# A hybrid block (window attention, RWKV-7, retention, FFN): norm factors moved to the keys, rotation in one product, in-context rate kept as its tanh, key scale on ScalarE

## Chip, cores and metric

One core of one Trainium2 chip. The metric is device time in microseconds (us) of one execution, the median of the runs shown. TensorE (PE) multiplies matrices, VectorE (DVE) and ScalarE (ACT) work elementwise, GpSimd (POOL) does a few small powers, SyncE (SP) issues the loads. A core has an on-chip memory of 128 partitions; TensorE writes its sums to PSUM.

## The reference

Two layers over 256 tokens of width 1024, float32. In each layer one projection feeds three branches, whose outputs are gated, mixed, projected and added to the input; a gated FFN follows. Cut to what the change touches:

```python
def hybrid_layer(x, ...):
    h = _rms(x) * norm1_g
    aq, ak, av, rw, rq, rk, rv, rg, gates = _split(h @ w_in, IN_SIZES)
    aq = _rms(aq.reshape(B, T, 8, 64)) * attn_q_norm_g      # 8 query heads
    ak = _rms(ak.reshape(B, T, 2, 64)) * attn_k_norm_g      # 2 key heads
    o_a = sliding_window_attention(aq, ak, av, attn_sinks) @ w_attn_o
    o_b = rwkv7_time_mix(rw, ...) @ w_rwkv_o
    o_c = retention(rq, rk, rv, rg) @ w_ret_o
    ...
def rwkv7_time_mix(h, ...):
    ...
    a = jax.nn.sigmoid(a0 + ad @ a2)                        # in-context rate
    kk = (k * k_k); kk = kk / max(norm_per_head(kk), 1e-12)
    k = k * (1.0 + (a - 1.0) * k_a)                         # key scale
    # per step: S = S*w + (S @ -kk) * (kk*a) + v*k ; y = S @ r
    ...
def _rotary(x, pos):                                        # on rq and rk
    x1, x2 = x[..., :32], x[..., 32:]
    return concat([x1 * cos - x2 * sin, x2 * cos + x1 * sin])
```

The attention's scores are products of a query and a key, so a factor per element of the head can stand on either of them. The sigmoid is written as 0.5 + 0.5 tanh of half its argument.

## The kernel before

**Tiling.** Tokens come in two halves of 128 (`t`). Every weight is brought in as a unit of 128 x 1024 numbers (`raw`, 512 KB), split by ScalarE into a rounded part `wh` and by VectorE into the rest `wl`, and multiplied in three products (high by high, high by low, low by high), which keeps float32 accuracy. Three buffers each hold `raw`, `wh` and `wl`.

**Streams.** The big products form one chain in program order (called bulk): attention's queries `aq` and keys and values `akv`, the rwkv columns `pf`, retention's `rq`, `rv`, `rg`, `rk`, the gates `gt`, the branches' output products `po` (attention, then retention, then rwkv), `px`, and the FFN's `pfg`, `pfu`, `pd`. Beside it run the attention (stream 3), the rest of rwkv (stream 1), the retention (stream 2) and the mixing (stream 4).

**Order.** Nothing is issued in program order. `Program` records every operation; `schedule` and `forward` simulate the five queues from a table of costs (`cost`) and latencies, and pick on each engine the ready operation with the highest key; `emit` then writes that order out, so all instructions carry line 432 in the profile and are told apart by their tiles. The key puts due weights first, then the longest remaining path (with the costs of stream 1 counted 2.5 times), and lets bulk products fill the rest. An engine works through its own queue strictly in order. The costs that meet the change:

```python
if eng == "DVE":
    ...
    if method in ("tensor_copy", "tensor_scalar", "memset") and not src:
        return 150 + n / 1.92
    return (210 if method == "scalar_tensor_tensor" else 150) + n / 0.96
if eng == "ACT":
    c = (155 if src else 200) + n / 1.2
    if _is_ap(kw.get("scale", 1.0)) or _is_ap(kw.get("bias", 0.0)):
        c += 95
```

**Buffers.** Tiles of a pool are handed out in program order: `s` (4 buffers of work space: `q_sb`, `asq`, `ask`, `qn`, `t1`, `t2` and others), `m` (5 buffers: the attention's `aqs`, `sc`, `pT`, then the retention's `rqT`, `rkT`, `sT`), `r` (14, mostly rwkv), `k` (5), and 4 PSUM buffers each for bulk and for the rest.

**Attention, for each t.** `q_sb` is the query, evicted from PSUM with the row's scale; ScalarE squares it, VectorE sums the squares per head, GpSimd raises them to -1/2 (`arq`). Two VectorE products write `qn`, the query times its norm's factor with the heads regrouped (pairs of a head of each key group side by side); TensorE transposes `qn` (`pta`). The keys get their row's factor and their norm's factor in `kv`. `qng` holds both norm factors of both layers, spread over the partitions by four loads. Scores `sc`, their maximum `amx`, the exponentials with their sums, the reciprocal `adn` of the denominator, the transposes `ptp` into `pT` and the product `poa` follow.

**Rotation.** `rope` evicts to `q_sb`, multiplies by cosines into `t1` (one product of 512) and by signed sines into `t2` (two products of 256, each reading the other half of every head); the sum is transposed into `rqT` or `rkT`. Then come `pst`, `sT`, `po`, the square `rsq`, its sums `rvr`, the power on GpSimd and its scale (`rrr`), two products `o`, and the transposes `ptc` into `och` and `ocl`, which the bulk product with `w_ret_o` reads.

**Rwkv.** `na` is the tanh of the in-context rate from ScalarE, turned by one VectorE operation of 1024 numbers a partition into minus the rate (-0.5 tanh - 0.5). After the key's norm (`kq`, `pss`, `ssm`, `rin`, `kkn`), four VectorE operations write `k2` = `na` * `nka` + `oka` (shown in the profile as `k`), then come `k2` * `zk`, `na` * `kkn`, the decays `EN`, the operands `X`, and a triangular inverse of 31 steps on VectorE (`prod`, `Tt`).

Of the kernel before, what the change touches and what calls it, by code (L numbers as in the profile page):

```python
# [439 lines left out]
def hybrid_kernel(ctx: ExitStack, tc: tile.TileContext, A: dict, cst_d: bass.AP, out: bass.AP, layers=L):  # L440
# [64 lines left out]
    def bcast_rows(src, n, o):  # L505
        return bass.AP(tensor=src.tensor, offset=src.offset + o, ap=[[0, 128], [1, n]])
# [142 lines left out]
    hw = TL(cp, [128, 16], F32, name="hw")  # L649
    ts(hw, vec[:, 28:44], 0.5, None, MUL)  # L650
    nka = TL(cp, [128, 8], F32, name="nka")
    ts(nka, vec[:, vo["ka"]:vo["ka"] + 8], -1.0, None, MUL)
    oka = TL(cp, [128, 8], F32, name="oka")
    ts(oka, vec[:, vo["ka"]:vo["ka"] + 8], -1.0, 1.0, MUL, ADD)
    qng = TL(cp, [128, 2, 2, 64], F32, name="qng")
    snk = TL(cp, [128, 16], F32, name="snk")
    for l in range(L):
        dma(out=qng[:, l, 0, :], in_=bcast_rows(A["attn_q_norm_g"], 64, l * 64))
        dma(out=qng[:, l, 1, :], in_=bcast_rows(A["attn_k_norm_g"], 64, l * 64))
    dma(out=snk, in_=bcast_rows(A["attn_sinks"], 16, 0))  # L660


# [7 lines left out]
    for l in range(layers):  # L670
# [23 lines left out]
        def rope(ps, t):  # L694
            q = ST([128, 512], "q_sb")
            act(q, ps[t], AF.Copy, scale=rs[:, t:t + 1])
            t1 = ST([128, 512], "t1")
            cosb = bc(C("cos")[:, t * 32:(t + 1) * 32].unsqueeze(1), [128, 16, 32])
            tt(t1.rearrange("p (a b) -> p a b", b=32), q.rearrange("p (a b) -> p a b", b=32), cosb, MUL)
            t2 = ST([128, 512], "t2")  # L700
            q4 = q.rearrange("p (h s b) -> p h s b", s=2, b=32)
            t24 = t2.rearrange("p (h s b) -> p h s b", s=2, b=32)
            for s in range(2):
                sinb = bc(C("sin")[:, t * 64 + s * 32:t * 64 + (s + 1) * 32].unsqueeze(1), [128, 8, 32])
                tt(t24[:, :, s, :], q4[:, :, 1 - s, :], sinb, MUL)
            return t1, t2

        def rope_T(ps, dstT, keep=None):
# [16 lines left out]
        for t in range(2):  # L725
            q = ST([128, 512], "q_sb")
            kv = TL(z_p, [128, 256], F32, tag="kv", name="kv")
            act(q, psq[t], AF.Copy, scale=rs[:, t:t + 1])
            act(kv, psk[t], AF.Copy, scale=rs[:, t:t + 1])
            av.append(kv)  # L730
            sq = ST([128, 512], "asq")
            ss = TL(sm_p, [128, 10], F32, tag="ass", name="ass")
            act(sq, q, AF.Square)
            V.tensor_reduce(out=ss[:, 0:8], in_=sq.rearrange("p (h v) -> p h v", h=8), axis=AX.X, op=ADD)
            sk = ST([128, 128], "ask")
            act(sk, kv[:, 0:128], AF.Square)
            V.tensor_reduce(out=ss[:, 8:10], in_=sk.rearrange("p (h v) -> p h v", h=2), axis=AX.X, op=ADD)

            ts(ss[:, 0:8], ss[:, 0:8], 64e-6, None, ADD)
            ts(ss[:, 8:10], ss[:, 8:10], 1.0 / 64, 1e-6, MUL, ADD)  # L740
            rq_ = TL(sm_p, [128, 10], F32, tag="arq", name="arq")
            G.tensor_tensor(out=rq_, in0=ss, in1=C("mh")[:, :10], op=ALU.pow)
            q3 = q.rearrange("p (h v) -> p h v", h=8)
            rqs.append(rq_)
            qn = ST([128, 512], "qn")
            qn4 = qn.rearrange("p (g k v) -> p k g v", g=4, k=2)
            for kvh in range(2):
                tt(qn4[:, kvh], q3[:, kvh * 4:kvh * 4 + 4, :], bc(qng[:, l, 0:1, :], [128, 4, 64]), MUL)
            k3 = kv[:, 0:128].rearrange("p (h v) -> p h v", h=2)
            tt(k3, k3, bc(rq_[:, 8:10].unsqueeze(2), [128, 2, 64]), MUL)  # L750
            tt(k3, k3, bc(qng[:, l, 1:2, :], [128, 2, 64]), MUL)
            pt = PS([128, 512], "pta")
            transposes(pt, qn)
            p4 = pt.rearrange("p (k t) -> p k t", k=4)
            for kvh in range(2):
                r_, q_ = HR[kvh], HR[1 - kvh]
                S.copy(qs[t][r_, kvh], p4[r_])
                tt(qs[t][q_, kvh], p4[r_], qs[t][r_, kvh].bitcast(F32), SUB)
            pt = PS([128, 128], "ptk")
            P.transpose(pt, kv[:, 0:128], ident)  # L760
            tk = slice(t * 128, (t + 1) * 128)
            for kvh in range(2):
                r_, q_ = HR[kvh], HR[1 - kvh]
                S.copy(ks[r_, kvh, tk], pt[r_])
                S.copy(ks[q_, kvh, tk], pt[r_])
                tt(klz[r_, kvh, tk], pt[r_], ks[r_, kvh, tk].bitcast(F32), SUB)
# [73 lines left out]
        for u in (6, 2, 3, 0, 1, 4, 5):  # L840
            pf = [PG([128, T], "pf") for _ in range(2)]
            for kg in range(2):
                wh, wl = wunit(w_in[kg * 512:(kg + 1) * 512, 768 + 256 * u:768 + 256 * (u + 1)], 4, 256)
                hh, hl = hts[kg]
                for f in range(2):
                    for k in range(4):
                        a, b = wh[:, k, f * 128:(f + 1) * 128], wl[:, k, f * 128:(f + 1) * 128]
                        fst, lst = (kg == 0 and k == 0), (kg == 1 and k == 3)
                        rec.bulk = True
                        mm(pf[f], a, hh[:, k, :], fst, False)  # L850
                        mm(pf[f], a, hl[:, k, :], False, False)
                        mm(pf[f], b, hh[:, k, :], False, lst)
                        rec.bulk = False
            rec.stream = 1
            rec.urgent = True
            for f in range(2):
                c = 2 * u + f
                hs = TL(z_p, [128, T], F32, tag="hs", name="hs")
                tt(hs, pf[f], RB, MUL)
                act(dst[c], hs, AF.Copy, scale=omu[:, l * 14 + c:l * 14 + c + 1])  # L860
                stt(dst[c][:, 1:], hs[:, 0:T - 1], vec[:, l * 14 + c:l * 14 + c + 1], dst[c][:, 1:], MUL, ADD)
            rec.urgent = False
            if u == 6:
                act(wa[0:64, :], wa[0:64, :], AF.Tanh)
                act(sg, sg, AF.Tanh, scale=0.5)
                ts(sg, sg, 0.5, 0.5, MUL, ADD)

                tw = RT([128, 4, T], "tw")
                na = RT([128, 4, T], "na")
                for i in range(2):  # L870
                    pw = PS([128, 2, T], "pw")
                    pa = PS([128, 2, T], "pa")
                    with rec.together(0.5):
                        for j in range(2):
                            p = 2 * i + j
                            mm(pw[:, j, :], wa2[0:64, p * 128:(p + 1) * 128], wa[0:64, :])
                            mm(pa[:, j, :], wa2[64:128, p * 128:(p + 1) * 128], wa[64:128, :])
                    for j in range(2):
                        p = 2 * i + j
                        act(tw[:, p, :], pw[:, j, :], AF.Tanh, scale=0.5, bias=hw[:, l * 4 + p:l * 4 + p + 1])  # L880
                        act(na[:, p, :], pa[:, j, :], AF.Tanh, scale=0.5, bias=hw[:, 8 + l * 4 + p:9 + l * 4 + p])
                ts(tw, tw, 1.0, None, ADD)
                ts(na, na, -0.5, -0.5, MUL, ADD)
                cum = RT([128, 4, T], "cum")
                for p in range(4):
                    V.tensor_tensor_scan(cum[:, p, :], C("scan"), tw[:, p, :], 0.0, MUL, ADD)
                EI = TL(r_p, [128, 4, 4, 65], F32, tag="r", name="EI")
                G.memset(EI[:, :, :, 0:1], 1.0)
                cum4 = cum.rearrange("p a (c t) -> p a c t", c=4)
                act(EI[:, :, :, 1:65], cum4, AF.Exp, scale=DECAY_C)  # L890
                EN = RT([128, 4, T], "EN")
                act(EN, cum, AF.Exp, scale=-DECAY_C)
                PC = TL(sm_p, [128, 4, 4], F32, tag="PC", name="PC")
                S.copy(PC, EI[:, :, :, 64])

            rec.stream = 0
# [11 lines left out]
        def rwkv_rest():  # L908
# [25 lines left out]
                    stt(kkn[:, p, :], zk[:, p, :], vcol("kk", p), pb[:, j, :], MUL, MUL)  # L934
            k2 = RT([128, 4, T], "k2")
            for p in range(4):
                ts(k2[:, p, :], na[:, p, :], nka[:, l * 4 + p:l * 4 + p + 1], oka[:, l * 4 + p:l * 4 + p + 1], MUL, ADD)
            tt(k2, k2, zk, MUL)
            tt(na, na, kkn, MUL)

            X = [None] * 4
            c4 = lambda ap: ap.rearrange("p (c t) -> p c t", c=4)
            for i in range(2):
                pp = slice(2 * i, 2 * i + 2)
                tt(na[:, pp], na[:, pp], EN[:, pp], MUL)
                tt(EN[:, pp], k2[:, pp], EN[:, pp], MUL)
            for p in range(4):
                X[p] = RT([128, 2, 4, 128], "X")
# [396 lines left out]
```

## Time and profile before

| | before |
|---|---|
| median of 3 runs | 991.02 us (990.52 to 991.4) |
| profiled execution | 990.79 us, its span 988.8 us |
| granted TensorE clock, mean | 0.99 |
| PE busy | 964.6 us, 98% of the span |
| DVE busy | 686.7 us, 69% |
| ACT busy | 522.8 us, 53% |
| POOL busy | 45.9 us, 5% |
| read from memory | 157.01 MB, 160 GB/s over the span |

Busy time is the time in which an engine has an instruction running; TensorE's matmuls overlap, so a busy TensorE need not be at its peak. The span runs from the first to the last instruction, and the execution's own time is a little longer. Lists of groups have the line, engine, operation, the tile written and those read, the shape, then count, busy time and the mean of one in ns, and the idle time before them with what ended it. Lists of waits have who waited for whom, the total in us, the number of waits and the longest.

### The profile page before, as it was taken

The page shows a single profiled execution, that of the slowest core. Times are in us where ns is not written, and L with a number is a line of the kernel's source. Part 1 is how long each engine was busy: PE and PEld are TensorE (multiplying, and loading weights), DVE is VectorE, ACT ScalarE, POOL GpSimd, SP SyncE. Part 2 cuts the span into 40 slices and gives each one's busy share as a digit, 9 for nine tenths or more (in the row PEclk, how much of TensorE's full clock was granted, in tenths as well). Part 3 has the DMA queues.
Part 4 walks back from the last instruction along what each step waited for, and adds up shares of the span by engine and source line. Part 5 has one row for each costly group of instructions (what it writes and reads, how often), then busy time and mean ns, then how long its engine had stood idle before and what let it go on. Part 6 is the DMA issues. An engine that isn't in the chain of part 4 may idle for free.

```text
span 988.8 us, 15098 instructions
## 1 busy us (share of the span) xinstructions
PE 964.6 (98%) x5894; PEld 800.7 (81%) x5894; DVE 686.7 (69%) x1066; ACT 522.8 (53%) x820; POOL 45.9 (5%) x37
## 2 busy tenths in 40 slices
PE   8999999979999999999999999997999999999998
PEld 6998787757888888898889987775778888888886
DVE  5888888867877555555468798878677765555443
ACT  7766756344446544444466765742535474444432
POOL 1101000010200000000010100001002000000000
PEclk9999999989999999999999999997999999999999
DMA  8555454513555666655554464444125556666562
GB/s 256 170 168 170 133 149 128 171 64 87 161 184 163 202 177 190 190 174 190 189 171 150 133 206 124 142 137 134 64 79 186 186 164 198 188 180 187 180 207 102
DMA packets 93265, 159.04 MB, mean 161 GB/s; under 512 B 5798, under 2 KB 26506, under 8 KB 93194
## 3 DMA queue, kind: packets, MB, share of 16 engines
q1 hardware_dynamic: 93194, 158.08, 52.9%
q8 instruction: 46, 0.75, 0.3%
q14 instruction: 25, 0.20, 0.1%
HBM read 157.01 MB, written 1.05 MB: 160 GB/s over the span
## 4 chain that ended last, share of the span: by engine, by line
PE 91%; DVE 2%; issue 2%; DMA 2%; POOL 1%; ACT 1%; SPq 0%; ACTq 0%; DVEq 0%; POOLq 0%
PE pd L432 13%; PE gt L432 12%; PE pfg L432 12%; PE pfu L432 12%; PE po L432 8%; PE pf L432 7%; PE px L432 4%; PE rk L432 2%; PE rg L432 2%; PE rv L432 2%; PE rq L432 2%; PE py L432 2%; DMA raw<-in_w_in_dram 1%; PE aq L432 1%; PE poa L432 1%
## 5 line engine op out<-in xcount | busy, mean ns | idle before, releaser
L432 DVE TENSOR_TENSOR wl<-raw,wh 128x1024 fp32r<-128x1024 f32 x292 | 356.7, 1222 | 203.0 <-ACT wh L432 202.1
L432 ACT CAST wh<-raw 128x1024 fp32r<-128x1024 f32 x292 | 306.1, 1050 | 307.2 <-PE pd L432 66.9
L432 PE MATMUL gt<-wh,htl 128*128 128x512 f32 x192 | 76.9, 400 | 0.0
L432 PE MATMUL gt<-wl,hth 128*128 128x512 f32 x192 | 76.5, 399 | 0.0
L432 PE MATMUL gt<-wh,hth 128*128 128x512 f32 x192 | 76.2, 397 | 0.0
L432 PE MATMUL pfg<-wl,hth 128*128 128x512 f32 (+1 forms) x192 | 72.6, 378 | 0.0
L432 PE MATMUL pfg<-wh,hth 128*128 128x512 f32 (+1 forms) x192 | 72.2, 376 | 0.0
L432 PE MATMUL pfg<-wh,htl 128*128 128x512 f32 (+1 forms) x192 | 71.6, 373 | 0.0
L432 PE MATMUL pfu<-wh,hth 128*128 128x512 f32 (+1 forms) x192 | 71.3, 371 | 0.0
L432 PE MATMUL pfu<-wl,hth 128*128 128x512 f32 (+1 forms) x192 | 71.3, 371 | 0.0
L432 PE MATMUL pfu<-wh,htl 128*128 128x512 f32 (+1 forms) x192 | 71.3, 371 | 0.0
L432 PE MATMUL pd<-wl,ath 128*128 128x512 f32 x176 | 69.6, 395 | 0.0
L432 PE MATMUL pd<-wh,atl 128*128 128x512 f32 x176 | 69.5, 395 | 0.0
L432 PE MATMUL pd<-wh,ath 128*128 128x512 f32 x176 | 69.4, 395 | 0.0
L432 PE MATMUL pf<-hth,wh 128*128 128x256 f32 x224 | 64.5, 288 | 0.0
L432 PE MATMUL pf<-hth,wl 128*128 128x256 f32 x224 | 63.9, 285 | 0.0
L432 PE MATMUL pf<-htl,wh 128*128 128x256 f32 x224 | 63.5, 284 | 0.0
L432 PEld LDWEIGHTS pf<-hth,wh 128*128 128x128 f32 x224 | 42.9, 192 | 0.7 <-issue 0.7
L432 PEld LDWEIGHTS pf<-hth,wl 128*128 128x128 f32 x224 | 42.9, 191 | 0.7 <-issue 0.7
L432 PEld LDWEIGHTS pf<-htl,wh 128*128 128x128 f32 x224 | 42.9, 192 | 0.0
L432 PEld LDWEIGHTS gt<-wh,hth 128*128 128x128 f32 x192 | 36.1, 188 | 8.0 <-issue 1.1
L432 PEld LDWEIGHTS gt<-wl,hth 128*128 128x128 f32 x192 | 36.1, 188 | 7.9 <-issue 0.8
(323 smaller groups left out, 1961.1 us busy)
## 6 DMA issues: line engine op xcount, KB each, us to landing
raw<-in_w_in_dram SPq DMA_DIRECT2D x120, 512.0 KB, 3.7
raw<-in_w_ffn_gate_dram SPq DMA_DIRECT2D x44, 512.0 KB, 3.7
raw<-in_w_ffn_up_dram SPq DMA_DIRECT2D x44, 512.0 KB, 3.7
raw<-in_w_ffn_down_dram SPq DMA_DIRECT2D x44, 512.0 KB, 3.6
raw<-in_w_out_dram SPq DMA_DIRECT2D x16, 512.0 KB, 3.5
raw<-in_w_attn_o_dram SPq DMA_DIRECT2D x8, 512.0 KB, 4.2
raw<-in_w_ret_o_dram SPq DMA_DIRECT2D x8, 512.0 KB
raw<-in_w_rwkv_o_dram SPq DMA_DIRECT2D x8, 512.0 KB, 3.7
```

The costliest lines, as they stand in the source:

```text
L432: fn(*args, **kw)
```

## The change

1. **Norm factors.** The query's factor is multiplied once, at the start, into the key's factor (`qng`), for both layers. `qn` and its two products for each `t` are gone; the query is evicted straight into the regrouped layout, the sums of its squares are read from that layout and written back in head order, and `pta` transposes `q_sb`.
2. **Rotation.** The two products that write `t2` become one over 512 numbers, which reads the halves of each head in reversed order.
3. **In-context rate.** `na` stays the tanh. The factor -0.5 and the added 1 move into three later products, which become three-operand operations: (`na` + 1) * `kkn`, then (`na` * -0.5) * `EN`.
4. **Key scale.** The four operations that write `k2` move from VectorE to ScalarE (Identity with a scale and a bias per partition); `nka` and `oka` are rescaled to fit.

```diff
-    ts(nka, vec[:, vo["ka"]:vo["ka"] + 8], -1.0, None, MUL)
+    ts(nka, vec[:, vo["ka"]:vo["ka"] + 8], 0.5, None, MUL)
-    ts(oka, vec[:, vo["ka"]:vo["ka"] + 8], -1.0, 1.0, MUL, ADD)
+    ts(oka, vec[:, vo["ka"]:vo["ka"] + 8], -0.5, 1.0, MUL, ADD)
...
         dma(out=qng[:, l, 1, :], in_=bcast_rows(A["attn_k_norm_g"], 64, l * 64))
+    tt(qng[:, :, 1, :], qng[:, :, 0, :], qng[:, :, 1, :], MUL)
...
-            for s in range(2):
-                sinb = bc(C("sin")[:, t * 64 + s * 32:t * 64 + (s + 1) * 32].unsqueeze(1), [128, 8, 32])
-                tt(t24[:, :, s, :], q4[:, :, 1 - s, :], sinb, MUL)
+            sinb = bc(C("sin")[:, t * 64:(t + 1) * 64].rearrange("p (s b) -> p s b", s=2).unsqueeze(1), [128, 8, 2, 32])
+            tt(t24, q4[:, :, ::-1, :], sinb, MUL)
...
-            act(q, psq[t], AF.Copy, scale=rs[:, t:t + 1])
+            act(q.rearrange("p (g k v) -> p k g v", g=4, k=2), psq[t].rearrange("p (k g v) -> p k g v", g=4, k=2),
+                AF.Copy, scale=rs[:, t:t + 1])
...
-            V.tensor_reduce(out=ss[:, 0:8], in_=sq.rearrange("p (h v) -> p h v", h=8), axis=AX.X, op=ADD)
+            V.tensor_reduce(out=ss[:, 0:8].rearrange("p (k g) -> p g k", k=2), in_=sq.rearrange("p (g k v) -> p g k v", g=4, k=2),
+                            axis=AX.X, op=ADD)
...
-            q3 = q.rearrange("p (h v) -> p h v", h=8)
             rqs.append(rq_)
-            qn = ST([128, 512], "qn")
-            qn4 = qn.rearrange("p (g k v) -> p k g v", g=4, k=2)
-            for kvh in range(2):
-                tt(qn4[:, kvh], q3[:, kvh * 4:kvh * 4 + 4, :], bc(qng[:, l, 0:1, :], [128, 4, 64]), MUL)
...
-            transposes(pt, qn)
+            transposes(pt, q)
...
                 ts(tw, tw, 1.0, None, ADD)
-                ts(na, na, -0.5, -0.5, MUL, ADD)
...
-                ts(k2[:, p, :], na[:, p, :], nka[:, l * 4 + p:l * 4 + p + 1], oka[:, l * 4 + p:l * 4 + p + 1], MUL, ADD)
+                act(k2[:, p, :], na[:, p, :], AF.Identity, scale=nka[:, l * 4 + p:l * 4 + p + 1], bias=oka[:, l * 4 + p:l * 4 + p + 1])
             tt(k2, k2, zk, MUL)
-            tt(na, na, kkn, MUL)
+            stt(na, na, 1.0, kkn, ADD, MUL)
...
-                tt(na[:, pp], na[:, pp], EN[:, pp], MUL)
+                stt(na[:, pp], na[:, pp], -0.5, EN[:, pp], MUL, MUL)
                 tt(EN[:, pp], k2[:, pp], EN[:, pp], MUL)
```

The order of all queues is planned anew from the new list of operations.

## The prediction, made before the result was known

> **What bounds the kernel now.** I read the page first (busy shares, slices, chain), then who waits for whom on TensorE, then busy time by stretch, then the chain inside the worst stretch.
>
> ```profile
> span 988.8 us, 15098 instructions
> PE 964.6 (98%) x5894; PEld 800.7 (81%) x5894; DVE 686.7 (69%) x1066; ACT 522.8 (53%) x820; POOL 45.9 (5%) x37
> PE   8999999979999999999999999997999999999998
> PE 91%; DVE 2%; issue 2%; DMA 2%; POOL 1%; ACT 1%; SPq 0%; ACTq 0%; DVEq 0%; POOLq 0%
> ```
>
> TensorE is the bound: 98% busy, 91% of the chain. No matmul is added or removed by this change, so only the places where TensorE is not busy can pay: 988.8 - 964.6 = 24.2 us. The slices show them: the start, one slice near 190 us and one near 690 us, one per layer. Those two are the same wait:
>
> ```profile
> PE ptc L432 <- DVE o L432: 11.8, 4, 5.7
> ...
> PE pta L432 <- DVE qn L432: 0.8, 1, 0.8
> ```
>
> The first row is the transpose of the retention's output (`ptc`), which waits for the product `o` on VectorE: 11.8 us in all. The second is the attention's query transpose behind the product with the norm's factor, 0.8 us, once. By stretch (columns: from:to, its length, then busy time and count of PE, PEld, DVE, ACT, POOL, then the granted clock, DMA share, GB/s):
>
> ```profile
> 40.00:180.00 140.00, 139.94 (x933) 117.02 (x932) 120.99 (x212) 88.00 (x162) 4.76 (x2) 1.00 0.52 151
> 80.00:110.00 30.00, 30.00 (x143) 24.80 (x142) 28.62 (x47) 20.54 (x42) 0.00 (x0) 1.00 0.64 183
> 198.00:204.00 6.00, 0.43 (x3) 0.12 (x2) 5.45 (x18) 0.60 (x1) 2.13 (x2) 0.73 0.18 70
> ...
> 568.00:598.00 30.00, 30.00 (x142) 24.88 (x141) 29.13 (x48) 20.45 (x40) 0.00 (x0) 1.00 0.65 191
> 674.00:694.00 20.00, 12.85 (x67) 10.40 (x66) 17.07 (x44) 5.06 (x7) 2.60 (x2) 0.70 0.40 127
> ```
>
> From 40 to 180 us TensorE never stops, so VectorE time saved there reaches the end only if it brings the retention forward. At 198 to 204 us TensorE has 0.43 us of work in 6.0: the next weights' product in the written order needs the retention's second half. At 80 to 110 us (and 568 to 598) VectorE itself is nearly full, 28.62 and 29.13 of 30. The chain through the hole, in order of time (start, length, what):
>
> ```profile
> 195.70 2.46 PE po L432 x20
> ...
> 200.39 1.74 POOL rrr L432
> ...
> 202.51 0.68 DVE o L432
> ...
> 204.15 1.09 PE ptc L432 x4
> ```
>
> It is a serial tail with little queueing in it: product, square, sum, power on GpSimd, two products, transpose. It gets shorter for TensorE only by starting earlier.
>
> **The change part by part.** VectorE's and ScalarE's groups (columns: count | busy us, mean ns):
>
> ```profile
> L432 DVE SCALAR_TENSOR_TENSOR tg<-tg,po 128x512 f32<-128x512 f32 x16 | 10.7, 680 | 1.0 <-PE po L432 0.8
> ...
> L432 DVE TENSOR_TENSOR t<-q_sb,cst 128x256 f32<-128x256 f32 x16 | 6.6, 412 | 2.0 <-PE ptr L432 2.0
> ...
> L432 DVE TENSOR_TENSOR t<-q_sb,cst 128x512 f32<-128x512 f32 x8 | 5.5, 682 | 1.0 <-ACT q_sb L432 1.0
> ...
> L432 DVE STREAM_TRANSPOSE Y<-GA 128x1024 f32<-128x1024 f32 x2 | 4.1, 2032 | 0.0
> ...
> L432 DVE TENSOR_TENSOR qn<-q_sb,qng 128x256 f32<-128x256 f32 x8 | 3.3, 420 | 0.0
> ...
> L432 DVE TENSOR_SCALAR k<-na,nka,oka 128x256 f32<-128x256 f32 x8 | 2.9, 406 | 0.0
> ...
> L432 DVE TENSOR_TENSOR na<-na,EN 128x512 f32<-128x512 f32 x4 | 2.7, 681 | 0.0
> ...
> L432 DVE TENSOR_SCALAR na<-na 128x1024 f32<-128x1024 f32 x2 | 1.4, 688 | 0.0
> ```
> ```profile
> L432 ACT COPY pT<-ptp 128x512 f32<-128x512 f32 x12 | 6.8, 585 | 6.5 <-PE ptp L432 6.5
> ...
> L432 ACT ACTIVATE zr<-hs,omu 128x256 f32<-128x256 f32 x8 | 4.1, 518 | 2.4 <-DVE hs L432 2.4
> ...
> L432 ACT ACTIVATE na<-pa,hw 128x256 f32<-128x256 f32 x8 | 3.4, 481 | 0.0
> ```
>
> All counts are for both layers; a layer has half.
>
> *Norm factors on the keys.* Four `qn` products a layer go: 4 x 0.420 = 1.68 us of VectorE. The query's eviction now writes its heads regrouped; `pT<-ptp`, an eviction that regroups its blocks in such a way, takes 585 ns for 512, which leaves nothing for the regrouping to have cost, so I price it at no change. The sum over squares keeps its size. One product of 128 elements is added at the start; `kv<-kv,qng` of that size and kind is the row for it:
>
> ```profile
> L432 DVE TENSOR_TENSOR kv<-kv,qng x4: 285/286/286, 35.2 to 525.2; 128x128 f32<-128x128 f32 x4
> ...
> DMA to landing us min/median/max: 3.6/4.0/4.4
> ```
> ```profile
> 30.01 0.51 SPq L432 DMA_DIRECT2D qng<-in_attn_k_norm_g_dram  x1
> ```
>
> So 0.29 us once. This product needs all four loads of `qng`, the last issued at 30.0 us and so landed by about 34.4, and its first reader stands at 35.2: no wait if it is put after 34.4, up to 4.4 us of a held-up VectorE queue (weights' second halves behind it) if it is put at 30. `qn` had stood at the head of the transposes `pta`; without it they need the eviction alone, 0.8 us of TensorE's wait gone in layer 0. What comes late next there is the first weights, so I take 0.8, with 0 as the other end.
>
> *Rotation.* 8 halves of 0.412 become 4 wholes. With the 512-element product of the same operands as the nearest row: 8 x 0.412 - 4 x 0.682 = 0.57 us saved a layer. A reversed order of the halves is in no row. The slowest rate in VectorE's rows is the block transpose, 2032 ns for 1024, or 1.02 us for 512: then 4 x 1.02 - 3.30 = 0.78 us lost. Nothing in the rows makes it under 0.68. I take 0.68, since the same tile is read there.
>
> *In-context rate as its tanh.* One `na` rescaling goes, 0.69 us a layer. Two products of 512 and one of 1024 become three-operand operations; 680 against 681 ns at 512 says nothing is added.
>
> *Key scale on ScalarE.* 4 x 0.406 = 1.62 us leave VectorE, 4 x 0.48 to 0.52, or 2.0 us, come to ScalarE, which has 9.5 us free in the 30 from 80 to 110. The Trainium skill, in "ScalarE: Activation LUTs", section "Rules for kernel authors", says multiplications and additions belong on VectorE because it is the faster one per element. The rows agree, 406 against 481 to 518 ns; by that rule the edit loses 4 x 0.1 = 0.4 us a layer, by the full VectorE queue it gains 1.62, and I go by the queue.
>
> VectorE loses 1.68 + 0.57 + 0.69 + 1.62 = 4.56 us a layer. What of it reaches the hole? The queue of the full stretch:
>
> ```profile
> 83.98 1.05 DVE L432 TENSOR_SCALAR k<-na,nka,oka 128x256 f32<-128x256 f32 x3
> ...
> 86.08 0.41 DVE L432 TENSOR_SCALAR k<-na,nka,oka 128x256 f32<-128x256 f32 x1
> ...
> 109.14 0.17 DVE L432 TENSOR_TENSOR adn<-adn,aes 128x8 f32<-128x8 f32 x1
> ...
> 111.09 0.37 DVE L432 TENSOR_TENSOR t<-q_sb,cst 128x256 f32<-128x256 f32 x1
> ```
>
> The attention's denominator `adn` stands behind all of the rwkv work of that stretch. The rest of the attention, then its five large buffers, then the retention's rotated queries and keys that take those buffers over, follow it. So the 1.62 us of `k2`, and 2 x 0.14 of the first rotation just behind it, come off the start of the retention: 1.9 us a layer. The other parts lie ahead of waits that swallow them (VectorE's waits from 40 to 190 us):
>
> ```profile
> DVE ssm L432 <- PE pss L432: 2.5, 1, 2.5
> ...
> DVE sc L432 <- PE pas L432: 1.7, 1, 1.7
> ```
>
> The scores `sc` cover the 1.68 of `qn`, the key norm's sum `ssm` covers the 0.69 of `na`. If these covers are gone, they count too (second rival). From 110 to 190 us I let the 1.9 through whole, because the steps release one another; the low end is 0.
>
> Sum: 0.8 + 2 x 1.9 = 4.6 us. The profiled execution took 990.79 us (span 988.8 and 2.0 around it); 990.79 - 4.6 = 986.2, and with the 0.23 by which the median of the three runs (991.02) lies above it, **986.4 us**.
>
> **The rivals.**
>
> *Nothing arrives.* The retention's transposes and products stand at written places in TensorE's queue, between weights' products; if these places stay, an earlier VectorE changes nothing. For it: TensorE's 139.94 of 140 us. Against it: in the hole the release is VectorE's `o`. Then only the wait at `pta` goes: 991.02 - 0.8 = 990.2 us.
>
> *The whole saving arrives, and the clock with it.* If all 4.56 us reach the hole, the wait shrinks from 5.7 to about 1.1 us. After the long wait TensorE's clock is low, the stretch behind the hole (columns as before):
>
> ```profile
> 204.00:208.00 4.00, 3.85 (x12) 3.24 (x13) 3.76 (x10) 0.59 (x1) 0.61 (x2) 0.55 0.02 4
> ```
>
> A granted clock of 0.55 over 4 us is 0.45 x 4 = 1.8 us of work lost while TensorE had all its inputs. So 2 x (4.56 + 1.8) + 0.8 = 13.5 us: 991.02 - 13.5 = 977.5. Against it: the two covers above. The Trainium skill, in "TensorE: Matmul & The Clock Gate", section "What's actually happening", puts the halving behind an idle window of about 3.4 us; by it a shift of 2.3 us would already spare the clock. The rows agree as far as they go, 0.73 within the hole of 5.7 us and 1.00 from 40 to 180; none of them has a wait of a length between the two.
>
> *Slower: the key scale is caught in ScalarE's queue.* ScalarE's waits from 76 to 112 us:
>
> ```profile
> ACT wh L432 <- PE rv L432: 3.4, 2, 1.8
> ACT wh L432 <- DMA raw<-in_w_in_dram: 3.1, 3, 1.7
> ```
> ```profile
> 86.47 1.05 ACT L432 CAST wh<-raw 128x1024 fp32r<-128x1024 f32 x1 [0.72 <-PE rq L432]
> ```
> ```profile
> 88.68 1.22 DVE L432 TENSOR_TENSOR k<-k,zk 128x1024 f32<-128x1024 f32 x1
> ```
>
> Weight casts `wh` wait at the head of that queue for TensorE to free a buffer or for a load, 6.5 us in five waits, 1.3 each. An `Identity` written behind one waits as long, and VectorE's product `k<-k,zk` waits for it with the weights' second halves queued behind. Four of them, one wait each: 5.2 us in place of 1.62, so 3.6 us later a layer, and TensorE's hole longer by that: 991.02 + 2 x 3.6 - 0.8 = 997.4. It decides from the point at which the last `Identity` ends after 88.7 us, where that product stands now. For it: ScalarE's scales become due just where these waits begin. Against it: the first of them after 80 us, 0.72, ends only at 86.5.
>
> **How the numbers follow.** Forecast (2 to 8 us gained) 0.38; whole saving 0.14; nothing 0.22; slower 0.26, of which 0.16 is the rival above and 0.10 a planned order that puts the retention later without that, which no row prices. The change in time that a measurement of this kernel tells from none is about 0.2%, 2 us. So faster 0.52, same 0.22, slower 0.26. The forecast's own range is 983 to 989. For 8 in 10 the range takes in the rivals' 977.5 and 997.4, with 2.5 us more below (layer 1's row has 20.00 - 12.85 = 7.2 us of idle TensorE to give, more than the 4.56 taken) and rounded above: 975 to 998.
>
> **What would show it.** `adn` first at about 107.3 us; `ptc` waiting for `o` about 8 us in all, the longest near 3.8; no wait of `pta` for VectorE; `t` only in 512-element operations of 0.68; the `Identity` rows near 0.50, the last ended by 86 us; VectorE 686.7 - 2 x 4.56 + 0.3 = 677.9 us busy, ScalarE 526.8, TensorE's idle time down by 4.6. The prediction is wrong if `adn` moves and `ptc` does not, if a new wait of `k` for ScalarE stands in VectorE's list, or if the order around the hole is another one.

## The result: 979.95 us, faster by 1.1%, more than twice what was forecast

| | before | after |
|---|---|---|
| median | 990.89 us (990.52 to 991.4) | 979.95 us (979.12 to 980.95) |
| ratio, 95% interval | | 0.989 (0.9873 to 0.9907) |
| profiled execution, its span | 990.79, 988.8 us | 980.18, 978.1 us |
| mean granted TensorE clock | 0.990 | 0.998 |

The forecast was 986.4 us, a gain of 4.6; measured are 10.9. The page of the kernel after, the lines that answer to those of before:

```profile
span 978.1 us, 15091 instructions
...
PE 962.3 (98%) x5894; PEld 797.7 (82%) x5894; DVE 679.3 (69%) x1041; ACT 526.1 (54%) x828; POOL 40.2 (4%) x37
...
PE   8999999999999999999999999999999999999998
...
PE 96%; DVE 1%; ACT 1%; issue 1%; DMA 0%; SPq 0%; POOL 0%; ACTq 0%; DVEq 0%; POOLq 0%
```

The two weak slices are gone, and the chain is 96% TensorE instead of 91%. TensorE's idle time falls from 24.2 to 978.1 - 962.3 = 15.8 us, its busy time from 964.6 to 962.3. Who TensorE waits for (total, times, longest):

```profile
PE po L432 <- ACT obh L432: 3.5, 2, 1.8
PE idle L432 <- POOL zero L432: 2.6, 1, 2.6
PE po L432 <- DVE ocl L432: 1.8, 2, 0.9
PE rq L432 <- DVE wl L432: 1.2, 2, 0.6
```

The wait of `ptc` for `o`, 11.8 us, stands nowhere in the list any more, nor does that of `pta`. New is the output product `po` waiting for rwkv's output `obh`. The stretches around the old hole (from:to, length, busy PE, PEld, DVE, ACT, POOL, granted clock, DMA share, GB/s):

```profile
198.00:204.00 6.00, 5.39 (x23) 4.43 (x24) 5.62 (x15) 2.11 (x2) 0.00 (x0) 1.00 0.31 92
204.00:208.00 4.00, 4.00 (x19) 3.30 (x18) 4.00 (x9) 1.06 (x1) 0.00 (x0) 1.00 0.41 131
...
674.00:694.00 20.00, 18.72 (x83) 14.81 (x82) 18.27 (x37) 8.13 (x10) 0.61 (x2) 1.00 0.50 156
```

5.39 us of TensorE work where there had been 0.43, at full clock where it had been 0.73 and 0.55. But the hole did not shrink because its tail came 1.9 us earlier. Three tiles' rows of layer 0 (minimum/median/maximum ns, then first and last start), of before:

```profile
L432 PE MATMUL pta<-cst,qn x8: 272/273/331, 30.9 to 36.5; 128*128 128x128 f32 x8
```
```profile
L432 PE MATMUL pst<-rqT,rkT x32: 272/272/373, 175.5 to 192.1; 64*128 64x128 f32 x32
```
```profile
L432 DVE TENSOR_TENSOR adn<-adn,aes x2: 159/164/169, 109.1 to 143.8; 128x8 f32<-128x8 f32 x2
```

and of after:

```profile
L432 PE MATMUL pta<-cst,q_sb x8: 272/272/273, 22.1 to 34.0; 128*128 128x128 f32 x8
```
```profile
L432 PE MATMUL pst<-rqT,rkT x32: 272/272/373, 154.6 to 170.2; 64*128 64x128 f32 x32
```
```profile
L432 DVE TENSOR_TENSOR adn<-adn,aes x2: 166/167/168, 97.5 to 131.8; 128x8 f32<-128x8 f32 x2
```

The attention's query transposes start 8.8 us earlier, its denominators 11.6, the retention's score products 20.9. An edit that takes 4.56 us of VectorE's work out of a layer cannot shift a tile by 20.9 us within the same order: the planner wrote another one.

### The profile page after: what moved, and what is told of

Same layout as the page of the kernel before. It is cut to its first block, busy times and chain, and to the rows that moved or that the text cites. A ratio compares the mean times of both kernels' runs of the same rounds, so it can differ in the third digit from the quotient of the medians.

```text
span 978.1 us, 15091 instructions
## 1 busy us (share of the span) xinstructions
PE 962.3 (98%) x5894; PEld 797.7 (82%) x5894; DVE 679.3 (69%) x1041; ACT 526.1 (54%) x828; POOL 40.2 (4%) x37
## 4 chain that ended last, share of the span: by engine, by line
PE 96%; DVE 1%; ACT 1%; issue 1%; DMA 0%; SPq 0%; POOL 0%; ACTq 0%; DVEq 0%; POOLq 0%
PE gt L432 14%; PE pd L432 13%; PE pfg L432 12%; PE pfu L432 12%; PE pf L432 8%; PE po L432 8%; PE px L432 4%; PE rk L432 2%; PE rg L432 2%; PE rv L432 2%; PE rq L432 2%; PE py L432 2%; PE aq L432 1%; PE akv L432 1%; PE poa L432 1%; PE ptf L432 1%
## 5 line engine op out<-in xcount | busy, mean ns | idle before, releaser
L432 PE MATMUL pfg<-wh,htl 128*128 128x512 f32 (+1 forms) x192 | 71.7, 373 | 0.0
L432 PEld LDWEIGHTS gt<-wh,htl 128*128 128x128 f32 x192 | 36.0, 188 | 7.8
```

The source lines that it names most:

```text
L432: fn(*args, **kw)
```

## The experiments

Three theories, with the letters that the expectations use. **Shorter work** (Q, the prediction's): the microseconds that leave VectorE's full stretch reach the hole. **Head** (H): without `qn` the attention's `pta` comes early and frees its PSUM buffers, and the whole front of the layer moves up. **Order** (P): the planner, given other costs and other readiness, writes another order, and the order makes the time. First the parts, each alone and planned anew, then orders and operations taken apart. All medians:

| kernel | what | median us (range) | ratio to before, 95% | mean clock |
|---|---|---|---|---|
| `only_norm` | before + norm factors | 981.31 (981.09 to 981.58) | 0.9897 (0.9882 to 0.9912) | 0.993 |
| `only_rope` | before + rotation | 986.09 (985.03 to 987.7) | 0.9946 (0.9929 to 0.9964) | 0.993 |
| `only_tanh` | before + rate as tanh | 987.51 (986.64 to 990.69) | 0.9963 (0.9953 to 0.9972) | 0.994 |
| `only_scale` | before + key scale on ScalarE | 1004.34 (1002.93 to 1005.72) | 1.0134 (1.0115 to 1.0152) | 0.979 |
| `no_norm` | after - norm factors | 987.0 (986.52 to 987.75) | 0.9962 (0.9947 to 0.9977) | 0.991 |
| `no_rope` | after - rotation | 983.28 (983.17 to 984.87) | 0.9921 (0.9905 to 0.9937) | 0.997 |
| `no_scale` | after - key scale | 978.87 (977.62 to 980.87) | 0.9875 (0.9859 to 0.9892) | 0.998 |
| `qn_early` | before, `qn` recorded earlier | 996.18 (995.76 to 998.14) | 1.0058 (1.0043 to 1.0073) | 0.975 |
| `late_pta` | after, `pta` held back | 993.45 (989.25 to 995.18) | 1.0023 (1.0007 to 1.0039) | 0.986 |
| `old_order` | after's work, before's order | 991.51 (990.25 to 992.5) | 1.0005 (0.9996 to 1.0015) | 0.990 |
| `old_early` | the same, key scale earlier | 990.97 (988.97 to 991.64) | 0.9997 (0.9987 to 1.0006) | 0.992 |
| `old_no_scale` | `no_scale`'s work, before's order | 990.79 (990.45 to 992.73) | 1.0001 (0.9992 to 1.0011) | 0.990 |
| `new_order` | before's work, after's order | 985.51 (984.81 to 986.22) | 0.994 (0.9926 to 0.9955) | 1.000 |
| `qn_new` | `no_norm`'s work, after's order | 982.68 (982.57 to 984.39) | 0.9916 (0.9897 to 0.9936) | 1.000 |
| `norm_new` | `only_norm`'s work, after's order | 982.82 (982.03 to 983.04) | 0.9911 (0.9896 to 0.9926) | 1.000 |

The median of before beside these runs lay between 990.7 and 991.9 us. The clock is that of the profiled execution; its mean leaves out the first microseconds, before the first record of the clock.

### Each part alone

The norm part, `only_norm`, is these lines of the change (with the query's regrouped eviction and sum of squares, as in its diff):

```diff
+    tt(qng[:, :, 1, :], qng[:, :, 0, :], qng[:, :, 1, :], MUL)
...
-                tt(qn4[:, kvh], q3[:, kvh * 4:kvh * 4 + 4, :], bc(qng[:, l, 0:1, :], [128, 4, 64]), MUL)
...
-            transposes(pt, qn)
+            transposes(pt, q)
```

> The norm factors on the keys alone (qn and its products gone), the other three parts as before. Theory H (head): the query's transposes pta no longer stand behind qn, start about 9 us earlier, and everything behind them in the layer with them, so this part alone gives most of the 10.9 us: 979 to 984 us. Theory Q (the full VectorE stretch from 80 to 110 us, as predicted): only the 0.8 us of the wait at pta: about 990. Theory P (any change makes the planner write another order, and this one happened to be good): no relation between this part's time and the whole's.

`only_rope`:

```diff
-            for s in range(2):
-                sinb = bc(C("sin")[:, t * 64 + s * 32:t * 64 + (s + 1) * 32].unsqueeze(1), [128, 8, 32])
-                tt(t24[:, :, s, :], q4[:, :, 1 - s, :], sinb, MUL)
+            sinb = bc(C("sin")[:, t * 64:(t + 1) * 64].rearrange("p (s b) -> p s b", s=2).unsqueeze(1), [128, 8, 2, 32])
+            tt(t24, q4[:, :, ::-1, :], sinb, MUL)
```

> The rotation's second product as one operation alone. Theory H: within 1.5 us of 991. Theory Q: 0.3 to 0.6 us a layer faster, about 990. Theory P: several us either way. The operation with the reversed halves: 0.68 us.

`only_tanh` (with the rescaled `nka` and `oka`):

```diff
-                ts(na, na, -0.5, -0.5, MUL, ADD)
...
-            tt(na, na, kkn, MUL)
+            stt(na, na, 1.0, kkn, ADD, MUL)
...
-                tt(na[:, pp], na[:, pp], EN[:, pp], MUL)
+                stt(na[:, pp], na[:, pp], -0.5, EN[:, pp], MUL, MUL)
```

> The rate kept as its tanh alone (the rescaling of na gone, three-operand products in its place, the key scale still on VectorE). Theory H: within 1.5 us of 991. Theory Q: the 0.69 us lies ahead of a wait and gives nothing, 990 to 991. Theory P: several us either way.

`only_scale`:

```diff
-                ts(k2[:, p, :], na[:, p, :], nka[:, l * 4 + p:l * 4 + p + 1], oka[:, l * 4 + p:l * 4 + p + 1], MUL, ADD)
+                act(k2[:, p, :], na[:, p, :], AF.Identity, scale=nka[:, l * 4 + p:l * 4 + p + 1], bias=oka[:, l * 4 + p:l * 4 + p + 1])
```

> The key scale on ScalarE alone, with before's na and factors. Theory H: within 1.5 us of 991. Theory Q: 1.6 us a layer off the full stretch, so 987 to 988, with adn 1.6 us earlier. Theory P: several us either way.

The parts give -10.2, -5.4, -4.0 and +12.8 us, -6.8 together; the whole gives -10.9. None stands near its own VectorE time over two layers (3.4, 1.1, 1.4 and 3.2 us). The part that the forecast counted on most, the key scale, alone makes the kernel slower by 1.3%. Its waits of TensorE, and two stretches behind the hole:

```profile
PE ptc L432 <- DVE o L432: 11.1, 2, 5.6
PE pz L432 <- DVE Tn L432: 6.5, 2, 3.4
PE gt L432 <- DVE rg_sb L432: 2.9, 2, 1.5
```
```profile
200.00:220.00 20.00, 13.72 (x156) 9.71 (x157) 9.38 (x20) 5.51 (x10) 1.76 (x3) 0.57 0.13 45
692.00:716.00 24.00, 17.55 (x171) 12.48 (x173) 10.99 (x20) 5.89 (x11) 1.70 (x3) 0.50 0.13 43
```

The hole stays, a wait for rwkv's triangular inverse (`Tn`) follows it in the new order, and the clock is at half through most of the first stretch and all of the second. `only_norm` is the opposite oddity: 10.2 us faster with the hole unchanged,

```profile
PE ptc L432 <- DVE o L432: 11.7, 2, 5.9
```

so its gain is not in the hole, and hardly in TensorE's idle time at all: of the 9.4 us between the spans (988.8 and 979.4), 8.3 are busy time (964.6 before).

```profile
PE 956.3 (98%) x5894; PEld 799.1 (82%) x5894; DVE 684.9 (70%) x1059; ACT 521.9 (53%) x820; POOL 42.5 (4%) x37
```

The same products, in another order, take TensorE less time. From the starts of one matmul to the next, the retention's 64-column products take 6.3 us in place of 9.1 and the attention's output products 7.3 in place of 9.8; the rest comes in pieces under 1 us, with less half clock (0.993).

### Parts taken out of the whole

`no_norm`, `no_rope` and `no_scale` are the kernel after with one of those hunks undone, planned anew.

> The changed kernel with the norm part undone (qn and its products back; rotation, tanh and key scale stay changed). Theory H (the head of the layer, through the transposes pta): 988 to 991 us. If the parts add up as they were measured alone (-5.4, -4.0, +12.8): about 995. Theory P (each list of operations gets its own order): neither has to hold.

> The kernel after with the rotation's second product in two halves again, planned anew. If the rotation's 0.28 us a product counts only where nothing else waits: 979 to 981 us, the same as the kernel after. If what it gave alone (5.4 us) is its own: 984 to 986 us.

> The kernel after with the key scale back on VectorE, planned anew. Order theory: the time follows the planned order and not the parts; norm, rotation and rate together give no long hole, 980 to 984 us, and the key scale adds little either way once the other parts are there, although alone it cost 12.8. Additive theory: the parts' own differences add, 991 - 10.2 - 5.4 - 4.0 = 971 us.

Undoing the norm part costs 7 us, the rotation 3.3 (between its two expectations), and the key scale nothing: `no_scale`'s median is 1.1 us below that of the kernel after, with intervals of the ratios that overlap (0.9859 to 0.9892 against 0.9873 to 0.9907), so it isn't shown to beat it. The additive theory's 971 us falls, and so does the key scale as a source of gain. `no_rope` has a hole again:

```profile
PE ptc L432 <- DVE o L432: 8.9, 2, 4.4
```

`pst` starts at 161.8 us in it, but its second half only at 186.7, against 154.6 and 169.3: the 0.57 us a layer that the rotation saves on VectorE do not do that; another order does.

### Is it the early `pta`?

`qn_early` removes no work; it only records the `qn` products right behind the query's eviction, so that their buffer is handed out before `ask`'s, which waits for the keys:

```diff
             act(q, psq[t], AF.Copy, scale=rs[:, t:t + 1])
+            q3 = q.rearrange("p (h v) -> p h v", h=8)
+            qn = ST([128, 512], "qn")
+            qn4 = qn.rearrange("p (g k v) -> p k g v", g=4, k=2)
+            for kvh in range(2):
+                tt(qn4[:, kvh], q3[:, kvh * 4:kvh * 4 + 4, :], bc(qng[:, l, 0:1, :], [128, 4, 64]), MUL)
```

> The kernel before, with the two qn products recorded right behind the query's eviction instead of behind the key's square, so that qn's work buffer is handed out before that of the key's square and nothing of qn waits for the keys. No work is removed. Theory H: the transposes pta start near 23 us instead of 30.9, and the time comes out like that of the norm part alone, 981 to 984 us. If the removed VectorE work is what pays: 991. Theory P: anything.

`late_pta` is the kernel after with the planner told that `pta` comes after the key's square:

```diff
             act(sk, kv[:, 0:128], AF.Square)
+            squared = len(rec.ops) - 1
...
+            rec.after = squared
             transposes(pt, q)
+            rec.after = None
```

> The changed kernel with all its savings, but the planner is told that the query's transposes pta come after the key's square (as they did before), so they start near 30 us again. Theory H: the gain is lost, 988 to 991 us. If the saved work pays: 980 to 982. Theory P: anything.

Held back, the whole gain is lost (993.45); brought forward without anything removed, the time gets worse (996.18), although `pta` starts at 23.7 us:

```profile
L432 DVE TENSOR_REDUCE amx<-sc x4: 674/948/1209, 95.7 to 125.5; 128x4 f32<-128x512 f32 x2, 128x4 f32<-128x1024 f32 x2
```

The scores' maximum stands at 95.7 us there (52.2 before, 41.3 after): the planner put other work between. So with a late `pta` the planner did not find the good order, and an early one does not bring it about. `only_norm` met the head theory's number, but the head theory alone does not carry the gain.

### The new work in the old order

`old_order` writes the kernel after's operations out in the order of before, each at its counterpart's place (the written list moves the line that all instructions carry to 581 or 582):

```diff
-        order = self.order = self.schedule()
+        order = self.order = np.frombuffer(zlib.decompress(base64.b85decode(OLD)), np.int16).tolist()
```

> The changed kernel's operations in the order that the planner wrote for the kernel before: each takes the place of the one that it replaces, the merged rotation product the place of the first half, nothing is planned anew. Theory Q (shorter work by itself, 1.9 to 4.6 us a layer into the hole): 982 to 987 us. Theory P (the order is what changed the time): 989 to 991, less only the wait at pta of 0.8.

991.51 us: nothing. VectorE has its 6 us less to do (680.5 busy) and TensorE's `ptc` waits as long as before. One objection: here the `Identity` operations stand where `k2` had stood, behind weight casts on ScalarE (start, length, what):

```profile
83.36 1.04 ACT L581 CAST wh<-raw 128x1024 fp32r<-128x1024 f32 x1
84.31 1.58 ACT L581 ACTIVATE k<-na,oka,nka 128x256 f32<-128x256 f32 x3
85.80 1.03 ACT L581 CAST wh<-raw 128x1024 fp32r<-128x1024 f32 x1
86.74 0.60 ACT L581 ACTIVATE k<-na,oka,nka 128x256 f32<-128x256 f32 x1
```

and VectorE's waits from 70 to 112 us, of before and of `old_order`, show what that costs:

```profile
DVE wl L432 <- ACT wh L432: 0.9, 2, 0.5
```
```profile
DVE wl L581 <- ACT wh L581: 3.2, 5, 1.2
```

2.3 us more: the key scale's 1.62 us eaten at once. This is the mechanism of the prediction's slower rival, 2.3 us of its 5.2. `old_early` takes the objection away: the four `Identity` operations go ahead of those casts, right behind the last `kq`, at 71.7 us. Its edit is that of `old_order` with another written list, which moves these four in each layer and nothing else:

```profile
70.12 1.69 ACT L581 ACTIVATE kq<-zk,vec 128x256 f32<-128x256 f32 x4
71.72 2.06 ACT L581 ACTIVATE k<-na,oka,nka 128x256 f32<-128x256 f32 x4
```

> The operations of the kernel after in the order of the kernel before, with the four Identity operations of the key scale placed right behind the key's last kq on ScalarE (near 72 us in layer 0) instead of behind the weight casts near 84 us. Shorter-work theory: now nothing on VectorE waits for them, adn comes at about 107.3 us instead of 109.0, the wait of ptc for o falls from 11.8 to about 8 us, 987 us. Order theory: with TensorE's places unchanged nothing arrives, 990 to 991.5 us; or ScalarE, late by its 2.2 us of new work, hands the weights' casts on later and VectorE waits for those, also 990 to 992.

`old_no_scale` leaves the key scale on VectorE, so that ScalarE gets nothing new; its operations are those of `no_scale`, in the order of before.

> Norm factors, rotation and rate as in the kernel after, the key scale left on VectorE, all in the order of the kernel before: VectorE has 2.94 us a layer less to do and no engine has anything new. Shorter-work theory by the forecast's own steps: the norm's and the rate's part are swallowed ahead of the hole, the rotation's 0.28 us and the wait at pta's 0.8 arrive, 989.5 us; if the covers do not hold, 991 - 2 x 2.94 - 0.8 = 984.3. Order theory: 990 to 991.5, the wait of ptc for o still 11 to 12 us.

990.97 and 990.79 us: nothing either. Where the shortened queue ends in `old_early` is seen in two lines of VectorE's timeline, of before and of `old_early` (in brackets the idle time before and what ended it):

```profile
99.15 0.75 DVE L432 SCALAR_TENSOR_TENSOR rv_sb<-rv,nrs,cst 128x512 f32<-128x512 f32 x1 [0.55 <-PE rv L432]
```
```profile
98.66 0.75 DVE L581 SCALAR_TENSOR_TENSOR rv_sb<-rv,nrs,cst 128x512 f32<-128x512 f32 x1 [1.21 <-PE rv L581]
```

Ahead of this the product `k<-k,zk` came 1.2 us earlier (87.52 for 88.68). Here VectorE waits for TensorE's product `rv`, and 0.66 us of it go. The rest, 0.5, is for the most part the 0.4 by which everything in that execution starts earlier, `pta` too (30.5 for 30.9). `pst` comes at 175.1 for 175.5, and the hole is as long:

```profile
PE ptc L581 <- DVE o L581: 12.1, 4, 5.7
```

The Trainium skill, in "PSUM — Partial Sum Buffer", section "Engine vs sequencer instructions", has VectorE's queue strictly first in, first out; the 1.21 us in which it stands at `rv_sb`, with work ready behind it (the next product, `X<-kkn,EI`, reads an `EI` written by 75.7 us), agree.

### The old work in the new order

`new_order` is the converse: all operations of before in after's order. What after does not have stands just ahead of its first reader (the rotation's second half beside its first). One buffer had to change:

```diff
-            qn = ST([128, 512], "qn")
+            qn = TL(z_p, [128, 4, 128], F32, tag="Rz", name="qn", bufs=1).rearrange("p a b -> p (a b)")
```

With it GpSimd's zeroing of that tile moves behind `qn`; TensorE's list of waits has none for it.

> The operations of the kernel before, all of them (the query's norm products, both halves of the rotation's second product, the rate's rescaling and the key scale on VectorE), in the order planned for the kernel after; each operation that the kernel after does not have stands on VectorE just ahead of its first reader, and the norm products' output has the buffer of a tile that is used later in the layer. Order theory: the order alone makes the gain, so 980 to 984 us, no long wait of ptc for o, the retention's first score product near 155 to 158 us, though VectorE has its 9 us more of work. Shorter-work theory: VectorE's 4.56 us a layer come back, so the hole comes back with them, 988 to 991 us.

985.51 us lies between both expectations: half of the gain (5.5 of 10.9) comes from the order alone, with 686.3 us of VectorE work as before. Its waits of TensorE:

```profile
PE rq L582 <- DVE wl L582: 3.7, 4, 1.2
PE po L582 <- ACT obh L582: 3.5, 2, 1.8
PE pta L582 <- DVE qn L582: 2.5, 4, 1.0
PE idle L582 <- POOL zero L582: 2.2, 1, 2.2
PE po L582 <- DVE ocl L582: 1.8, 2, 0.9
```

The four waits that are no start-up add up to 11.5 us, as much as the hole had, but the smaller waits of before are fewer, and none here is longer than 1.8 us. TensorE's busy time is that of before, 964.7 for 964.6, so the 4.4 us between the two spans are all idle time (24.2 to 19.7):

```profile
PE 964.7 (98%) x5894; PEld 798.9 (81%) x5894; DVE 686.3 (70%) x1066; ACT 522.4 (53%) x820; POOL 40.3 (4%) x37
```

That needs a word, since the mean clock is 1.000 for 0.990. Before ran at half clock in two stretches behind its holes:

```profile
200.80:207.60 6.80, 3.45 (x11) 2.88 (x12) 6.39 (x19) 0.59 (x1) 1.93 (x3) 0.50 0.01 2
682.10:695.70 13.60, 8.13 (x31) 7.15 (x32) 10.72 (x32) 1.18 (x2) 2.34 (x3) 0.50 0.21 75
```

TensorE was busy in 3.45 + 8.13 = 11.6 us of them, so by estimate 5.8 us of work were lost. `new_order` has no such stretch, but the other products take about as much longer in sum: `rg` has 408 to 414 ns in place of 391 to 396, and the start is slow. Two pairs of neighbours from its first products `aq`:

```profile
13.36 0.63 PE L582 MATMUL aq<-wh,htl 128*128 128x512 f32 x1
13.79 0.63 PE L582 MATMUL aq<-wh,hth 128*128 128x512 f32 x1
...
14.71 0.39 PE L582 MATMUL aq<-wh,hth 128*128 128x512 f32 x1
14.93 0.39 PE L582 MATMUL aq<-wl,hth 128*128 128x512 f32 x1
```

Up to about 14 us they start 0.43 us apart, then 0.23: half speed at the start of this execution, which its mean clock does not show.

What of the gain is still missing here? Two of the waits are smaller in the kernel after: `rq` for `wl` 1.2, `pta` for `qn` gone. That is 2.5 + 2.5 = 5.0 of the 6.3 us between the two spans. The last two runs put back one each. `qn_new` has the `qn` products and nothing else of the old work, `norm_new` everything but them, both in after's order with the edits above.

> The order of the kernel after and its operations, but with the query's norm products back on VectorE just ahead of the transposes pta (their output in the buffer of a later tile); rotation, rate and key scale as in the kernel after. If the second half of the gain is the norm products' place ahead of pta: most of the 5.5 us come back, 983 to 985 us, pta waiting for qn 2 to 2.5 us in all, rq waiting for wl near 1.2. If it is VectorE's full stretch: 980 to 981.5 us.

> The order of the kernel after with the norm factors on the keys and nothing else of the change: rotation in halves, the rate rescaled, the key scale on VectorE. If the second half of the gain is the norm products' place: 980 to 981.5 us. If it is VectorE's full stretch, behind which rq waits for wl (3.7 us with all the old work, 1.2 in the kernel after): rq waits 3 to 4 us again, 982.5 to 985 us.

```profile
PE pta L582 <- DVE qn L582: 2.8, 4, 1.0
...
PE rq L582 <- DVE wl L582: 1.2, 2, 0.6
```
```profile
PE rq L582 <- DVE wl L582: 3.7, 4, 1.2
```

The first fence is `qn_new`, the second `norm_new`. They take 2.7 and 2.9 us more than the kernel after, 5.6 together, and `new_order` costs 5.5 more: within one order the edits add, as far as ratios that are uncertain by some 0.2%, 2 us each, can tell. Their intervals overlap with that of the kernel after, so the split rests on the medians and on the two waits, which come back one by one. Neither side of the expectation was right alone; by the medians it is about half each.

So the 10.9 us are: 5.5 the order; about 2.7 the norm products ahead of `pta`; about 2.8 the VectorE work ahead of the weights that `rq` reads (rotation, rate and key scale together; no run takes them apart in this order). The last two show only in the new order: in the old one all the edits together give 0, as far as 0.1% can tell.

## Why the prediction was wrong, by its own steps

- **What bounds the kernel: right as to the engine.** TensorE is the bound, and the two holes are gone. But "only the places where TensorE is not busy can pay" is wrong: its busy time depends on the order too. It fell by 2.3 us of the 10.7 between the spans in the kernel after, and by 8.3 of 9.4 in `only_norm`.
- **The wait at `pta`, 0.8 us: right and too narrow.** It is gone, but the edit's weight was in what an earlier `pta` lets the planner do (22.1 for 30.9 us), which no term of the sum priced.
- **Durations: mostly right.** The groups after, VectorE's and then ScalarE's (count | busy us, mean ns):

```profile
L432 DVE TENSOR_TENSOR t<-q_sb,cst 128x512 f32<-128x512 f32 x16 | 10.9, 680 | 3.5 <-PE ptr L432 2.9 <-ACT q_sb L432 0.6
...
L432 DVE SCALAR_TENSOR_TENSOR na<-na,EN 128x512 f32<-128x512 f32 x4 | 2.7, 685 | 0.0
...
L432 DVE TENSOR_TENSOR qng<-qng 128x128 f32<-128x128 f32 x1 | 0.3, 279 | 0.0
```
```profile
L432 ACT ACTIVATE k<-na,oka,nka 128x256 f32<-128x256 f32 x8 | 4.3, 590 | 0.0
```

  The reversed halves take 680 ns as taken, the three-operand products cost nothing more, the extra product at the start 0.28 us. The `Identity` was mis-sized, 590 ns for 480 to 520: the rows that it was priced by had one operand per partition, this one has two. VectorE's 679.3 and ScalarE's 526.1 us stand against 677.9 and 526.8.
- **The step that failed: "the 1.62 us of `k2`, and 2 x 0.14 of the first rotation just behind it, come off the start of the retention".** I took VectorE at 28.62 of 30 us as the pace of that stretch. It is not: its queue stands at `rv_sb` for TensorE, and what is saved ahead of it turns into a longer wait there. In the old order the low end, 0, was the truth, and the rival "nothing arrives" (990.2) is what three runs measured (990.8 to 991.5). The row that said so was in VectorE's list of waits, 0.55 us before `rv_sb`, and I passed over it because it was small: here a small wait for the bounding engine near the end of a full stretch was the sign that the filled queue was not the bound.
- **The order: priced on one side only.** A new order was given 0.10, as a loss. It is half of the gain here and a loss of 12.8 us for the key scale alone. The sentence that the prediction is wrong "if the order around the hole is another one" is what came true: `adn` at 97.5 us instead of 107.3, `ptc`'s wait gone instead of 8 us.
- **The covers.** "The scores `sc` cover the 1.68 of `qn`" held in the old order. In the new one `qn` stands ahead of `pta` with nothing over it and costs 2.5 to 2.8 us of waiting.
- **The rivals.** The nearest number was "the whole saving and the clock", 977.5, for its second half: the clock came back (0.990 to 0.998). Its first half, the saving reaching the hole, did not happen, so that the measured time lies near 977.5 is luck. The slower rival's mechanism is real (`old_order`, 2.3 us of waiting on VectorE) and cost no time, since VectorE was not the pace there; in the kernel after, the `Identity` operations run from 71.4 us, ahead of those casts.

What stays open: why the planner's choices come out as they do for each part, and why TensorE gets through the same products 8.3 us sooner in `only_norm`, with its hole unchanged. Nor is it known what the order's 5.5 us would be without the clock: the half clock of before cost some 5.8 us by the estimate above, other products cost about as much more in the new order, and no run changed the clock alone.

## What to carry to other kernels

Where an edit makes a planner write a new order, the edit's own microseconds are the smaller question: run the new work in the old order and the old work in the new order, and the two together say what each is worth. A queue that is 95% full need not be the pace: look whether something in it waits for the bounding engine. Here one short wait took back most of what was saved ahead of it. And parts timed alone did not add under replanning, while within one fixed order they did, to within the 2 us that could be told.

## What the runs showed of the hardware

**Half clock outlasts its cause.** In `only_scale` TensorE's granted clock was 0.50 through the 24 us from 692 to 716. Two waits reach into them, 5.6 us for `o` until 695.1 and 3.4 us for `Tn` until 700.4; from there on TensorE was busy without a gap, and still at half clock:

```profile
700.40:716.00 15.60, 15.60 (x165) 11.19 (x167) 3.01 (x4) 5.30 (x10) 0.00 (x0) 0.50 0.11 35
```

The Trainium skill, in "TensorE: Matmul & The Clock Gate", section "What's actually happening", gives full clock back after one busy window of about 3.4 us. The 15.6 us do not agree; what else the clock waits for there, no run here tells.

`qn_early`, whose longest waits are 5.2 and 6.7 us, has the lowest mean clock of all runs, 0.975. Where no wait in the middle of the kernel was over 1.8 us (`new_order`, `qn_new`, `norm_new`) the mean clock was 1.000, and 0.998 in the kernel after. The 0.002 there are one stretch at half clock, from 545.7 to 549.1 us, and the longest wait in the 15 us ahead of it is 0.4 us: a long wait is not the only thing that such a stretch can follow.

**Two operands per partition on ScalarE.** An operation of 128x256 with both scale and bias per partition took 590 ns in the mean in the kernel after (`k<-na,oka,nka`), against 481 with a bias (`na<-pa,hw`) and 518 with a scale alone (`zr<-hs,omu`) in the kernel before.
